# Seven products of quarters for one pair of up-projection columns in four of eight MLP groups, and a planner that writes the order of groups 1 to 6

## The chip, the cores and the metric

The kernel runs on one core of one Trainium2 chip. The metric is the time of one execution in device microseconds (us); shown are the median of three runs and one more run under the hardware profiler.

## The reference, cut to what matters

Two layers work on a residual stream of 512 tokens by 1024 channels in float32. Layer 0 mixes tokens with attention, layer 1 with a short convolution. Each then has the MLP that the change is about, and a gated embedding.

```python
D_MODEL = 1024; SEQ = 512; D_FF = 4 * D_MODEL; DEPTH = 2

def sq_relu_mlp(h, w_up, w_down):
    return jnp.square(jax.nn.relu(h @ w_up)) @ w_down

for i in range(DEPTH):
    ...                                       # mixer, residual
    f = sq_relu_mlp(rmsnorm(x, g[2]), w_mlp_up[i], w_mlp_down[i])
    x = x + rmsnorm(f, g[3])
    ...                                       # gated embedding, residual
```

## The kernel before

**Products.** Each float32 operand is kept as two fp32r halves, a high one (names that end in `h`) and a low one (`l`, the operand minus its high half). `mm3` makes a product from three TensorE matmuls: high by high, low by high, high by low. The normed activations of the MLP stand transposed in SBUF as `hTh` and `hTl`, 8 blocks of 128 channels by 512 tokens.

**Weights.** A weight tile of 128 x 512 comes from HBM into a `raw` buffer (14 of them; SP's queue issues the transfers in the order of one list). ACT casts it to its high half (`wh<-raw`), and DVE or POOL subtracts to get the low half (`wl<-raw,wh`). `prepare` does this for the next 8 entries (`SOON`) of the list `order` ahead of the product that is being written.

**The MLP** of a layer is `mlp`: the 4096 hidden columns go in 8 groups of 512. `up(gr)` makes four blocks `f` of 128 columns, each from 8 x `mm3` over 512 tokens (24 matmuls of 512 columns) into one PSUM bank. ACT then applies relu (`r<-up`) and squares (`q<-r`). `down(gr)` adds the group's share of the down-projection for groups 0 to 6 with Strassen's seven products in Winograd's form. The left operands are quarters of the squared activations and their sums (A11, A12, A22, S1 to S4), of which `quarters` makes the sums on POOL (`s<-q`), and `halves` the high and low halves on ACT and DVE (for blocks 0 and 1, p = 0, and for blocks 2 and 3, p = 1). The right operands are quarters of the weights and their sums (B11, B21, B22, T1 to T4); for groups 1 to 6 DVE makes the sums T in PSUM banks (`dn_T<-...`). Each of the seven products fills two banks (`dn`, 12 matmuls of 512 columns in all), which DVE adds to 14 accumulators in SBUF (`acc<-dn,acc`). `combine` adds these up on POOL after group 6. Group 7 has plain products.

**Seven products elsewhere.** The conv of layer 1 already uses the seven-product form for two of its three projections (`sevens`): there the quarters of the tokens (B11 to B22, T1 to T4) are the moving operand, 256 columns wide, and quarter sums of the weight (S1 to S4, names `c_S`, `b_S`) the stationary one. A pair of 128-column blocks then takes 7 x 4 `mm3`, that is 84 matmuls of 256 columns, where `up` takes 48 of 512.

**Order.** The program writes instructions in the order of its loops, and a scheduler with a timing model of its own then orders each engine's queue, TensorE's (PE's) too. Each engine works its queue in order and waits on semaphores for others.

Of the kernel before, what the change touches and what calls it, by code (L numbers as in the profile page):

```python
# [8 lines left out]
F32 = mybir.dt.float32  # L9
F32R = mybir.dt.float32r  # L10
# [5 lines left out]
P = 128  # L16
# [22 lines left out]
BY_HAND = 8  # L39
LEFT = 10  # L40
LATE = 0
BANKED_FORMS = (
    ("B11", 0), ("T1", 0), ("B11", 1), ("T2", 0), ("B21", 0), ("T4", 0), ("T1", 1), ("T2", 1),
    ("B21", 1), ("T4", 1), ("T3", 0), ("T3", 1), ("B22", 0), ("B22", 1),
)
BANKED = range(1, 7)
DOWN_FORMS = ("B11", "T1", "B21", "T2", "T4", "T3", "B22")
# [16 lines left out]
low_on_pool = lambda key: key[0] == "up"  # L64


class Pair:


    def __init__(self, hi, lo):  # L70
        self.hi, self.lo = hi, lo
# [6 lines left out]
def trunk(ctx: ExitStack, tc, x, xT, pT, g, gT, wv, wqk, bf, wo, wci, wcq, cw, wco, wup, wdn, wpp, wpg, out):  # L78
# [3 lines left out]
    raws = pool("raws", RAWS)  # L82
    normed = pool("normed", 1)
    pages = pool("pages", PAGES)
    small = pool("small", 8)
# [44 lines left out]
    def plan_down(l, gr):  # L130

        plan_sums(
            ("dn", l, gr),
            [
                (PRODUCTS[i][1], p) for i in STEPS for p in range(2)
            ] if gr not in BANKED else BANKED_FORMS,
            [
                ((name, p), wdn[l, c, 4 * gr + 2 * p + r])
                for name, r, c in (("B11", 0, 0), ("B21", 1, 0), ("B12", 0, 1), ("B22", 1, 1))
                for p in range(2)  # L140
            ],
            [
                ((name, p), (a, p), (b, p), ALU.subtract)
                for p in range(2)
                for name, a, b in (("T1", "B12", "B11"), ("T3", "B22", "B12"),
                                   ("T2", "B22", "T1"), ("T4", "B21", "T2"))
            ],
        )

    def plan_sevens(key, srcs):  # L150
        plan_sums(
            key,
            [(f,) for f in QUARTERS],
            [((name,), src) for name, src in zip(("A11", "A12", "A21", "A22"), srcs)],
            [
                ((name,), (a,), (b,), op)
                for name, a, b, op in (
                    ("S1", "A21", "A22", ALU.add), ("S2", "S1", "A11", ALU.subtract),
                    ("S3", "A11", "A21", ALU.subtract), ("S4", "A12", "S2", ALU.subtract),
                )  # L160
            ],
        )
# [80 lines left out]
    for l in range(2):  # L243
        if l == 0:
            for c, (_, width) in enumerate(V_CHUNKS):
                for k in range(KT * width // 512 if width < 272 else KT):
                    plan(("v", c, k), wv[c][k])
            for i in range(KT):
                for j in range(4):
                    plan(("qk", i, j), wqk[i, j])  # L250
            for k in range(KT):
                for n in range(2):
                    plan(("o", n, k), wo[n, k])
        else:
            for s, key in enumerate((("cu", 0), ("b", 0), ("cu", 1))):
                for j in range(4):
                    plan((*key, j), wci[s, j])
            for i in range(2, KT, 2):
                for name in "ucb":
                    s = "cub".index(name)  # L260
                    if name in SEVENS:
                        plan_sevens((name, i), [wcq[i // 2 - 1, s, j] for j in range(4)])
                    else:
                        for j in range(4):
                            plan((name, i, j), wcq[i // 2 - 1, s, j])
            for n in range(2):
                for k in range(KT):
                    plan(("co", n, k), wco[n, k])
        for gr in range(8):
            for i in range(2):  # L270
                for j in range(4):
                    plan(("up", l, 2 * gr + i, j), wup[l, 2 * gr + i, j])
            if gr < 7:
                plan_down(l, gr)
                continue
            for n in range(2):
                for f in range(4):
                    plan(("dn", l, gr, n, f), wdn[l, n, 4 * gr + f])
        for k in range(2):
            plan(("p", l, k), pT[l, :, k, :])  # L280
        for n in range(2):
            for k in range(2):
                plan(("pp", l, n, k), wpp[l, n, k])
        for n in range(2):
            for k in range(KT):
                plan(("pg", l, n, k), wpg[l, n, k])
# [706 lines left out]
    def mlp(l, hT, xs, then, late):  # L993
        acc, lows = {}, {}

        def square(out, r):
            nc.scalar.activation(out, r, AF.Square)  # L997
# [41 lines left out]
        def down(gr, A):  # L1039

            for i in STEPS:
# [9 lines left out]
                for s in range(2):  # L1051
# [3 lines left out]
                    else:  # L1055
                        a = acc[i, s][:, :S]
                        ins = nc.vector.tensor_tensor(out=a, in0=banks[s], in1=a, op=ALU.add)  # L1057
                        if gr == 1:
# [4 lines left out]
                                ),  # L1063
                            )

        def combine():

            for s in range(2):
                for to, i in ((2, 1), (6, 1), (7, 6), (4, 7), (6, 5), (3, 6), (5, 7)):
                    a = acc[to, s][:, :S]  # L1070
                    nc.gpsimd.tensor_tensor(out=a, in0=a, in1=acc[i, s][:, :S], op=ALU.add)  # L1071
            return {
                (2 * half + s, n): acc[i, s]
                for s in range(2) for i, half, n in ((2, 0, 0), (3, 0, 1), (4, 1, 0), (5, 1, 1))
            }

        for gr in range(7):
            A, s, q = {}, {}, {f: page(f"q{l}_{gr}_{f}") for f in range(4)}

            def done(f, lo, hi, r):  # L1080
                square(q[f][:, lo:hi], r[:, : hi - lo])
                if lo == 0 and f % 2 == 0:
                    halves(gr, f, ("A11",), q[f], A)
                if hi == S:
                    quarters(gr, f, q, s, A)

            up(gr, done)
            down(gr, A)

        total, hs, gB = combine(), [], []  # L1090

# [203 lines left out]
def layout(x, p, norm_g, w_attn_in, b_forget, w_attn_out, w_conv_in, conv_w, w_conv_out,  # L1295
           w_mlp_up, w_mlp_down, w_ple_proj, w_ple_gate):

    import numpy as np

    def tiles(w, k, c):  # L1300

        K, C = w.shape
        t = w.reshape(K // (P * k), k, P, C // c, c).transpose(3, 0, 2, 1, 4)
        return t.reshape(C // c, K // (P * k), P, k * c)

    wa = np.asarray(w_attn_in)[0]
# [24 lines left out]
    got["wco"] = tiles(np.asarray(w_conv_out)[0], 1, S)  # L1331
    up, dn = np.asarray(w_mlp_up), np.asarray(w_mlp_down)
    got["wup"] = np.stack([tiles(up[l], 2, 256) for l in range(2)])
# [22 lines left out]
```

## Time and profile before

| | |
|---|---|
| median of 3 runs | 1220.68 us (1220.53 to 1222.57) |
| the profiled execution | 1221.12 us; its span from the first to the last instruction 1219.4 us |
| granted TensorE clock | 0.998 |
| busy: PE, DVE, ACT, POOL | 1206.7, 919.7, 691.0, 512.1 us |
| groups 1 to 6 of the MLP, each | about 40.8 us, in both layers |

Busy time is the time in which an engine has an instruction under way. Matmuls overlap, so their rate is read from the distance of their starts and not from their durations. Consecutive DVE and ACT instructions overlap in the record by about 0.1 us too.

### The profile page before, as it was taken

What the parts mean: (1) busy time and instruction counts of PE and PEld (TensorE: products, weight loads), DVE (VectorE), ACT (ScalarE), POOL (GpSimd) and SP (SyncE); (2) the same over time, 40 slices, a digit from 0 to 9 for tenths busy, and PEclk for the clock granted to TensorE, in tenths of its full rate; (3) what the DMA queues carried; (4) which work ended last, traced back from release to release, by engine and by line L of the source; (5) the groups of instructions that cost most, each with busy time, mean ns of one, the idle gap of its engine ahead of it and who ended that gap; (6) DMA issues with size and microseconds to landing.
All of it is one profiled execution on the core that took longest, in us unless ns stands there. A gap on an engine that the chain in (4) does not pass through costs nothing.

```text
span 1219.4 us, 18413 instructions
## 1 busy us (share of the span) xinstructions
PE 1206.7 (99%) x6175; PEld 1027.7 (84%) x6175; DVE 919.7 (75%) x1570; ACT 691.0 (57%) x1465; POOL 512.1 (42%) x520
## 2 busy tenths in 40 slices
PE   9999999999999999999999999999999999999997
PEld 8888887898888888888889999989888888888886
DVE  7888888584767866799877888866587678669873
ACT  7687778458644554455666533545755445545551
POOL 2035666155534543445213355226554345436210
PEclk9999999999999999999999999999999999999999
DMA  9476554623323423348223123542342234235501
GB/s 324 132 211 170 167 149 126 209 98 88 110 85 112 135 64 105 113 120 286 76 91 111 31 84 105 170 158 70 109 134 72 93 112 138 67 98 175 179 12 58
DMA packets 87310, 150.80 MB, mean 124 GB/s; under 512 B 10352, under 2 KB 18080, under 8 KB 87216
## 3 DMA queue, kind: packets, MB, share of 16 engines
q1 hardware_dynamic: 86640, 149.11, 39.3%
q8 instruction: 48, 0.79, 0.3%
q10 hardware_dynamic: 576, 0.53, 0.1%
q14 instruction: 46, 0.38, 0.1%
HBM read 139.03 MB, written 6.37 MB: 119 GB/s over the span
## 4 chain that ended last, share of the span: by engine, by line
PE 88%; ACT 3%; issue 3%; DVE 2%; POOL 2%; DMA 2%; SPq 0%; POOLq 0%; ACTq 0%; DVEq 0%
PE up L306 9%; PE up L304 9%; PE up L305 9%; PE dn L304 8%; PE dn L306 8%; PE dn L305 8%; PE v L512 3%; PE pg L305 2%; PE pg L304 2%; PE pg L306 2%; PE qk L306 2%; PE qk L305 2%; PE qk L304 2%; PE pT L626 1%; PE co L305 1%
## 5 line engine op out<-in xcount | busy, mean ns | idle before, releaser
L313 DVE TENSOR_TENSOR wl<-raw,wh 128x512 fp32r<-128x512 f32 x250 | 229.5, 949 | 21.3 <-ACT wh L312 20.4
L306 PE MATMUL up<-hTl,wh 128*128 128x512 f32 (+1 forms) x576 | 209.7, 366 | 1.0 <-DVE hTl L313 1.0
L304 PE MATMUL up<-hTh,wh 128*128 128x512 f32 (+1 forms) x576 | 210.3, 366 | 0.0
L305 PE MATMUL up<-hTh,wl 128*128 128x512 f32 (+1 forms) x576 | 210.2, 365 | 0.0
L312 ACT CAST wh<-raw 128x512 fp32r<-128x512 f32 x346 | 193.1, 630 | 4.5 <-DVE xd L409 4.4
L313 POOL TENSOR_TENSOR wl<-raw,wh 128x512 fp32r<-128x512 f32 x96 | 141.0, 1504 | 57.3 <-ACT wh L312 50.0
L306 PEld LDWEIGHTS up<-hTl,wh 128*128 128x128 f32 x576 | 108.3, 189 | 18.7 <-DVE hTl L313 1.2
L305 PEld LDWEIGHTS up<-hTh,wl 128*128 128x128 f32 x576 | 108.6, 189 | 17.6
L304 PEld LDWEIGHTS up<-hTh,wh 128*128 128x128 f32 x576 | 108.6, 189 | 17.5
L312 ACT CAST wh<-dn_T 128x512 fp32r<-128x512 f32 x112 | 61.9, 593 | 100.4 <-DVE dn_T L183 90.0
L1057 DVE TENSOR_TENSOR acc<-dn,acc 128x512 f32<-128x512 f32 x168 | 107.3, 678 | 8.2 <-PE dn L306 8.0
L1011 ACT ACTIVATE r<-up 128x512 f32<-128x512 f32 (+1 forms) x72 | 39.6, 551 | 121.9 <-PE up L306 121.9
L1025 POOL TENSOR_TENSOR s<-q 128x256 f32<-128x256 f32 x28 | 28.2, 1008 | 141.5 <-ACT q L997 139.5
L313 DVE TENSOR_TENSOR wl<-dn_T,wh 128x512 fp32r<-128x512 f32 x112 | 74.6, 692 | 9.4 <-ACT wh L312 9.1
L313 DVE TENSOR_TENSOR A12l<-q,A12h 128x512 fp32r<-128x512 f32 x28 | 19.4, 692 | 73.0 <-ACT A12h L312 73.0
L1071 POOL TENSOR_TENSOR acc<-acc,acc 128x512 f32<-128x512 f32 x28 | 46.5, 1682 | 23.7 <-DVE acc L1057 23.4
L306 PE MATMUL qk<-hTl,wh 128*128 128x512 f32 x128 | 50.6, 396 | 0.0
L305 PE MATMUL pg<-wh,hTl 128*128 128x512 f32 x128 | 50.5, 394 | 0.0
L304 PE MATMUL pg<-wh,hTh 128*128 128x512 f32 x128 | 50.4, 394 | 0.0
L304 PE MATMUL qk<-hTh,wh 128*128 128x512 f32 x128 | 50.3, 393 | 0.0
L305 PE MATMUL qk<-hTh,wl 128*128 128x512 f32 x128 | 50.2, 392 | 0.0
L306 PE MATMUL pg<-wl,hTh 128*128 128x512 f32 x128 | 50.2, 392 | 0.0
(406 smaller groups left out, 3330.6 us busy)
## 6 DMA issues: line engine op xcount, KB each, us to landing
raw<-in_wup SPq DMA_DIRECT2D x128, 256.0 KB, 3.2
raw<-in_wdn SPq DMA_DIRECT2D x128, 256.0 KB, 2.7
raw<-in_wcq SPq DMA_DIRECT2D x36, 256.0 KB, 3.1
raw<-in_wqk SPq DMA_DIRECT2D x32, 256.0 KB, 5.4
raw<-in_wpg SPq DMA_DIRECT2D x32, 256.0 KB, 5.3
g<-in_g SPq DMA_DIRECT2D x22, 256.0 KB, 6.3
prl<-neg_c SPq DMA_DIRECT2D x16, 256.0 KB, 6.3
raw<-in_wo SPq DMA_DIRECT2D x16, 256.0 KB, 4.8
```

The costliest lines, as they stand in the source:

```text
L304: nc.tensor.matmul(ps, a.hi, b.hi, start=start, stop=False)
L305: nc.tensor.matmul(ps, a.lo, b.hi, start=False, stop=False)
L306: nc.tensor.matmul(ps, a.hi, b.lo, start=False, stop=stop)
L312: nc.scalar.copy(hi, src)
L313: return eng.tensor_tensor(out=lo, in0=src, in1=hi.bitcast(F32), op=ALU.subtract)
L512: nc.tensor.matmul(ps[:, : V_CHUNKS[c][1]], getattr(of_x(k, t), p), getattr(ready["v", c, k], of), start=k == 0 and p == of, stop=k == KT ...
L626: nc.tensor.transpose(ps[:, b * P : (b + 1) * P], probs[h][b][:, j * P : (j + 1) * P], ident)
L1011: nc.scalar.activation(r[:, :n], ps[:, :n], AF.Relu)
L1025: sums = lambda out, a, b, op: nc.gpsimd.tensor_tensor(out=out, in0=a, in1=b, op=op)
L1057: ins = nc.vector.tensor_tensor(out=a, in0=banks[s], in1=a, op=ALU.add)
L1071: nc.gpsimd.tensor_tensor(out=a, in0=a, in1=acc[i, s][:, :S], op=ALU.add)
```

## The change

Groups 1 to 6 of each MLP are no longer written by `up` and `down`. A new function, `planned`, enters every step (a product on PE, a cast on ACT, a difference or sum on DVE or POOL, a transfer) into an `Agenda` with a cost, the steps it comes after and, for PE, the clock at which it is due. `Agenda.emit` then lets the engines run against each other by these costs. PE's steps keep their order of entry; on the other engines, of the steps that can start, the one that is due first goes first. The steps are written in that order under `manual_schedule` for PE, DVE, ACT and POOL, so the scheduler no longer orders them. PE's products stand strictly one after the other.

In groups 3 to 6 the first pair of blocks (f = 0 and 1) is made by seven products of quarters (`up_sevens`). Its results come as halves of three banks a, b and c, which DVE adds up (d, v, e, m). The token sums T1 to T4 for it are made once in each layer on POOL from `hT`, and split by ACT and DVE (`tokens_of_sevens`); they are kept in 7 new SBUF pages (`EXTRA`) and 9 of the 70 old ones. The four weight sums for each pair are made on POOL.

For groups 1 to 6 the order in which the down weights come changes too, and T3 is made as T2 minus B11 (one input in PSUM) where it was B22 minus B12 (two inputs in SBUF).

The core of the diff:

```diff
+UP_SEVENS = [(gr, 0) for gr in range(3, 7)]
+UP_PRODUCTS = (
+    ("A11", "B11", "c", 0), ("S2", "T2", "a", 1), ("S1", "T1", "b", 0), ("S3", "T3", "b", 1),
+    ("A12", "B21", "a", 0), ("S4", "B22", "c", 0), ("A22", "T4", "c", 1),
+)
+EXTRA = 7
+LOOK = 14.0
+LOOK_SUMS = 20.0
+SUM_BANKS = 3
+HOP = 0.25
+MARGIN = 2.0
+COSTS = {
+    "PE": (0.0, 0.0), "DVE": (0.07, 1.06e-3), "ACT": (0.17, 0.73e-3), "POOL": (0.15, 2.5e-3),
+    "DMA": (0.0, 1.9e-3),
+}
...
-                for name, a, b in (("T1", "B12", "B11"), ("T3", "B22", "B12"),
+                for name, a, b in (("T1", "B12", "B11"),
+                                   ("T3", "T2", "B11") if gr in BANKED else ("T3", "B22", "B12"),
                                    ("T2", "B22", "T1"), ("T4", "B21", "T2"))
...
+            while any(queues.values()):
...
+                for step in queue[:1] if e in ("PE", "DMA") else queue:
...
+                t = max(free[e], min(r for r, _ in ready))
+                step = min((s for r, s in ready if r <= t + 1e-9), key=lambda s: s.due)
+                wait = max(0.0, port - t) if step.shared else 0.0
...
+            def squared(gr, f, q, name, src, after, uses=()):
...                                       # ACT: relu, then Square
+            def up_sevens(gr, i, A):
...
+                        for k in range(4):
+                            w = ready[(*key, form)].at(lambda u: u[:, k * P : (k + 1) * P])
+                            mm3(ps[s][:, (L, R)[h]], w, second(tokens, k), k == 0, k == 3)
...
+                    at[n] = pe(12 * 0.12, product, [(*key, form)], after, new)
...                                       # after the first product: ACT copies bank c's left half to u
+                d = dve(S, sum_d, (at[4], at["u"]), [rooms["a"]])
+                v = dve(S, sum_v, (d, at[3]))
+                e = dve(256, sum_e, (v,), [rooms["b"]])
+                m = dve(S, sum_m, (v, at[6]), [rooms["c"]])
...
+            def up_plain(gr, i, A):
...
+                        step = pe(6 * 0.227, chunk, [(*key, j)], (), [room] if j == 0 else [])
...
+            def down_planned(gr, A):
+                for i in STEPS:
...
+                        step = pe(6 * 0.227, product, [("dn", l, gr, b_name, p)],
+                                  [low_of[gr, a_name, p]], rooms if p == 0 else [])
...
+            with tc.manual_schedule(engines={
+                mybir.EngineType.PE, mybir.EngineType.DVE, mybir.EngineType.Activation,
+                mybir.EngineType.Pool,
+            }):
+                agenda.emit()
...
-        for gr in range(7):
-            A, s, q = {}, {}, {f: page(f"q{l}_{gr}_{f}") for f in range(4)}
...
+        up(0, done)
+        down(0, A)
+        planned(range(1, 7))
```

**PE, start of the down-projection of group 6, layer 0, before.** In the names, `dn0_6_20` is layer 0, group 6, product 2, bank 0; `A12h0_6_3` is the quarter of blocks 2 and 3 that waits for the last up block (f = 3).

```order
L304 MATMUL dn0_6_50_6670<-wh209_6383,S1h0_6_1_6460 128x512
L305 MATMUL dn0_6_50_6670<-wh209_6383,S1l0_6_1_6461 128x512
L306 MATMUL dn0_6_50_6670<-wl209_6384,S1h0_6_1_6460 128x512
L304 MATMUL dn0_6_50_6670<-wh214_6493,S1h0_6_3_6560 128x512
L305 MATMUL dn0_6_50_6670<-wh214_6493,S1l0_6_3_6561 128x512
L306 MATMUL dn0_6_50_6670<-wl214_6494,S1h0_6_3_6560 128x512
L304 MATMUL dn0_6_20_6600<-wh216_6570,A12h0_6_3_6552 128x512
L305 MATMUL dn0_6_20_6600<-wh216_6570,A12l0_6_3_6553 128x512
```

**The same place now** (the quarter's name is `A12h0_6_2`).

```order
L420 MATMUL dn0_6_20_6960<-wh227_6703,A12h0_6_0_6855 128x512
L421 MATMUL dn0_6_20_6960<-wh227_6703,A12l0_6_0_6856 128x512
L422 MATMUL dn0_6_20_6960<-wl227_6704,A12h0_6_0_6855 128x512
L420 MATMUL dn0_6_21_6961<-wh227_6703,A12h0_6_0_6855 128x512
L421 MATMUL dn0_6_21_6961<-wh227_6703,A12l0_6_0_6856 128x512
L422 MATMUL dn0_6_21_6961<-wl227_6704,A12h0_6_0_6855 128x512
L420 MATMUL dn0_6_20_6960<-wh231_6722,A12h0_6_2_6957 128x512
L421 MATMUL dn0_6_20_6960<-wh231_6722,A12l0_6_2_6958 128x512
```

The second A12 product stood 30 matmuls behind the first down matmul of the group, after half of product 5; now it stands 18 behind.

**ACT, after the last up block of group 6, layer 0, before.** `r` and `q` are relu and square; A12h, S1h, S3h are high halves of left operands, `wh` those of weights.

```order
L1011 ACTIVATE r0_6_3_0_6549<-up0_6_3_0_6524 128x512
L997 ACTIVATE q0_6_3_6353<-r0_6_3_0_6549 128x512
L312 CAST A12h0_6_3_6552<-q0_6_3_6353 128x512
L312 CAST S1h0_6_3_6560<-s120_6_3_6556 128x512
L312 CAST S3h0_6_3_6564<-s340_6_2_6522 128x512
L312 CAST wh216_6570<-raw175_6361 128x512
```

**ACT at the same place now.**

```order
L1315 ACTIVATE rr0_6_3_6940<-up0_6_3_6865 128x512
L1515 CAST wh236_6942<-raw182_6655 128x512
L1319 ACTIVATE qr0_6_3_6951<-rr0_6_3_6940 128x512
L1515 CAST wh237_6954<-raw183_6674 128x512
L1265 CAST A12h0_6_2_6957<-qr0_6_3_6951 128x512
L1515 CAST wh238_6969<-raw184_6684 128x512
L1515 CAST wh239_6975<-raw185_6706 128x512
```

Two weight casts for group 7 now stand between the relu of the last block and the cast of A12 (one in groups 1, 3, 4 and 5, two in groups 2 and 6), and the weights of the group's own products are cast earlier.

**DVE, while group 3 of layer 0 makes its up blocks, before.** `dn_0_3_T2_0` is a weight sum, `wl` a low half of a weight.

```order
L1057 TENSOR_TENSOR acc0_3_1_4308<-dn0_2_31_5099,acc0_3_1_4308 128x512
L313 TENSOR_TENSOR wl145_5182<-dn_0_3_T2_0_5179,wh145_5181 128x512
L183 TENSOR_TENSOR dn_0_3_T4_0_5255<-raw126_5135,dn_0_3_T2_0_5179 128x512
L183 TENSOR_TENSOR dn_0_3_T1_1_5267<-raw129_5141,raw125_5133 128x512
L313 TENSOR_TENSOR A11l0_3_0_5195<-q0_3_0_5126,A11h0_3_0_5194 128x256
```

**DVE at the same place now.** `T3l`, `T4l` are low halves of the token sums, `up_0_6_S4` a weight sum of the seven products; d and v are sums of their results.

```order
L1208 TENSOR_TENSOR acc0_3_1_4311<-dn0_2_31_5206,acc0_3_1_4311 128x512
L1208 TENSOR_TENSOR T3l0_0_4807<-T3f0_0_4804,T3h0_0_4806 128x512
L1208 TENSOR_TENSOR T3l0_1_4823<-T3f0_1_4820,T3h0_1_4822 128x512
L1208 TENSOR_TENSOR wl139_5187<-up_0_6_S4_5153,wh139_5186 128x512
L1208 TENSOR_TENSOR T4l0_0_4882<-T4f0_0_4879,T4h0_0_4881 128x512
L1208 TENSOR_TENSOR T4l0_1_4909<-T4f0_1_4906,T4h0_1_4908 128x512
L1208 TENSOR_TENSOR wl145_5260<-raw124_4970,wh145_5259 128x512
L1208 TENSOR_TENSOR d0_3_0_5333<-up0_3_0a_5243,u0_3_0_5256 128x512
L1208 TENSOR_TENSOR dn_0_3_T1_0_5335<-raw125_5018,raw124_4970 128x512
L1208 TENSOR_TENSOR v0_3_0_5349<-up0_3_0b_5266,d0_3_0_5333 128x512
```

DVE now has eight more instructions in each of groups 3 to 6 (52 where it had 44): four low halves of weight sums and the four sums d, v, e, m. ACT has 43 where it had 38, POOL 19 where it had 16.

More of the change, by code (lines that the diff above doesn't have):

```diff
@@ L84, in trunk @@
     pages = pool("pages", PAGES)
+    extra = pool("extra", EXTRA)
     small = pool("small", 8)
@@ L138, in plan_down @@
                 ((name, p), wdn[l, c, 4 * gr + 2 * p + r])
+                for name, r, c, p in (
+                    ("B11", 0, 0, 0), ("B12", 0, 1, 0), ("B11", 0, 0, 1), ("B22", 1, 1, 0),
+                    ("B21", 1, 0, 0), ("B12", 0, 1, 1), ("B21", 1, 0, 1), ("B22", 1, 1, 1),
+                )
+            ] if gr in BANKED else [
+                ((name, p), wdn[l, c, 4 * gr + 2 * p + r])
                 for name, r, c in (("B11", 0, 0), ("B21", 1, 0), ("B12", 0, 1), ("B22", 1, 1))
@@ L270, in trunk @@
             for i in range(2):
+                tiles = [wup[l, 2 * gr + i, j] for j in range(4)]
+                if (gr, i) in UP_SEVENS:
+                    plan_sevens(("up", l, 2 * gr + i), tiles, UP_FORMS)
+                    continue
                 for j in range(4):
-                    plan(("up", l, 2 * gr + i, j), wup[l, 2 * gr + i, j])
+                    plan(("up", l, 2 * gr + i, j), tiles[j])
             if gr < 7:
@@ L1075, in combine, with done @@
             }
-        for gr in range(7):
-            A, s, q = {}, {}, {f: page(f"q{l}_{gr}_{f}") for f in range(4)}
[L1080 to L1088, printed above, removed]
+        A, s, q = {}, {}, {f: page(f"q{l}_0_{f}") for f in range(4)}
+        def done(f, lo, hi, r):
+            square(q[f][:, lo:hi], r[:, : hi - lo])
+            if lo == 0 and f % 2 == 0:
+                halves(0, f, ("A11",), q[f], A)
+            if hi == S:
+                quarters(0, f, q, s, A)
+        up(0, done)
+        down(0, A)
+        planned(range(1, 7))
         total, hs, gB = combine(), [], []
@@ L1332, in layout @@
     up, dn = np.asarray(w_mlp_up), np.asarray(w_mlp_down)
-    got["wup"] = np.stack([tiles(up[l], 2, 256) for l in range(2)])
+    plain = np.stack([tiles(up[l], 2, 256) for l in range(2)])
+    sevens = up.reshape(2, 2, 4, P, FF // 256, 2, P).transpose(0, 4, 5, 1, 3, 2, 6)
+    is7 = np.array([(i // 2, i % 2) in UP_SEVENS for i in range(FF // 256)])
+    got["wup"] = np.where(is7[:, None, None, None], sevens.reshape(plain.shape), plain)
     got["wdn"] = np.stack([tiles(dn[l], 1, S) for l in range(2)])
```

342 lines of the change are left out of this document (338 added, 4 removed).

## Prediction

> **What bounds the kernel now.** The page comes first: PE is busy for 99% of the span and carries 88% of the chain that ended last.
>
> ```profile
> PE 1206.7 (99%) x6175; PEld 1027.7 (84%) x6175; DVE 919.7 (75%) x1570; ACT 691.0 (57%) x1465; POOL 512.1 (42%) x520
> PE 88%; ACT 3%; issue 3%; DVE 2%; POOL 2%; DMA 2%; SPq 0%; POOLq 0%; ACTq 0%; DVEq 0%
> ```
>
> That is an average, so the second view is busy time by stage. The columns are the stretch, its length, then busy us of PE, PEld, DVE, ACT and POOL. The rows are the end of group 0 with up of group 1, two whole groups, down of group 6 with up of group 7, and group 1's down in layer 1.
>
> ```profile
> 295.00:324.40 29.40, 28.84 (x128) 23.57 (x127) 18.17 (x25) 20.41 (x39) 17.18 (x15) 1.00 0.43 118
> 406.10:446.90 40.80, 40.80 (x182) 33.76 (x181) 29.32 (x46) 20.81 (x39) 19.07 (x16) 1.00 0.33 104
> 487.80:528.60 40.80, 40.80 (x181) 33.75 (x181) 29.32 (x45) 20.82 (x39) 19.07 (x16) 1.00 0.34 104
> 528.60:569.40 40.80, 40.80 (x182) 33.78 (x181) 40.80 (x48) 24.35 (x47) 23.22 (x14) 1.00 0.67 216
> 892.00:933.00 41.00, 40.53 (x179) 33.57 (x180) 29.91 (x44) 20.17 (x38) 19.01 (x16) 1.00 0.34 103
> ```
>
> In a steady group PE never stops and nothing else is full: DVE has 11.5 us idle, ACT 20, POOL 21.7. So new order alone has nothing to win there, and fewer columns on PE shorten the kernel by as much, if the others keep up. The third view, what PE waits for, has in the MLP's groups 1 to 6 only this (us in all, times, longest; one in each layer):
>
> ```profile
> PE dn L304 <- ACT wh L312: 1.1, 2, 0.6
> ```
>
> **Part 1: 48 wide matmuls become 84 narrow ones.** The price is the distance of starts. First and last row of an up pair of 48 wide ones (the last is the first matmul of the next pair), then of a seven-product set in the conv, 84 narrow ones, up to the first of the next set:
>
> ```profile
> 420.06 0.39 PE L304 MATMUL up<-hTh,wh 128*128 128x512 f32 x1
> 430.94 0.39 PE L304 MATMUL up<-hTh,wh 128*128 128x512 f32 x1
> ...
> 693.77 0.28 PE L304 MATMUL c_A<-hTh,wh 128*128 128x256 f32 x1
> 703.84 0.28 PE L304 MATMUL b_A<-hTh,wh 128*128 128x256 f32 x1
> ```
>
> 10.88 us against 10.07 us, so 226.7 and 119.9 ns for each matmul. A pair saves 0.81 us; four groups in two layers make 8 x 0.81 = 6.5 us, all on PE's path. A group of that kind takes 40.8 - 0.8 = 40.0 us. [...]
>
> **Part 2: the wait that goes.** In group 1's down-projection PE stands for a weight cast that ACT has behind the casts of S1 and S3, which wait for POOL:
>
> ```profile
> 322.01 0.62 ACT L312 CAST S1h<-s 128x512 fp32r<-128x512 f32 x1 [1.35 <-POOL s L1025]
> 322.83 0.62 ACT L312 CAST S3h<-s 128x512 fp32r<-128x512 f32 x1 [0.20 <-POOL s L1025]
> 323.36 0.61 ACT L312 CAST wh<-raw 128x512 fp32r<-128x512 f32 x1
> 324.02 0.50 PE L304 MATMUL dn<-wh,A12h 128*128 128x512 f32 x1 [0.56 <-ACT wh L312]
> ```
>
> That weight is now cast while group 1's second up block is made. 2 x 0.56 = 1.1 us go, unless the next late thing takes the place, and that is part 3.
>
> **Part 3: PE can no longer go around a late operand.** The second A12 product stands 18 matmuls behind the first down matmul, 18 x 0.227 = 4.08 us, where it stood 30, 6.8 us. Its chain runs from the last up block over relu, square and cast on ACT to the low half on DVE. The rows of group 3 (first down matmul of PE, then the chain), and five casts in a row as the price of a cast put in between:
>
> ```profile
> 401.00 0.39 PE L304 MATMUL dn<-wh,A11h 128*128 128x512 f32 x1
> 401.20 0.60 ACT L1011 ACTIVATE r<-up 128x512 f32<-128x512 f32 x1 [0.82 <-PE up L306]
> 402.49 0.63 ACT L312 CAST A12h<-q 128x512 fp32r<-128x512 f32 x1
> 403.15 0.69 DVE L313 TENSOR_TENSOR A12l<-q,A12h 128x512 fp32r<-128x512 f32 x1 [0.97 <-ACT A12h L312]
> 402.54 0.74 POOL L1025 TENSOR_TENSOR s<-q,q 128x256 f32<-128x256 f32 x1 [1.25 <-ACT q L997]
> 407.77 2.72 ACT L312 CAST wh<-raw 128x512 fp32r<-128x512 f32 x5
> ```
>
> The low half is done at 403.84, 2.84 us behind 401.00, so 1.24 us are left. A cast costs (2.72 - 0.62) / 4 = 0.53 us. With one in between (groups 1, 3, 4, 5) 0.71 us remain, with two (2 and 6) 0.18. Lower bound of the new wait: 0. Upper bound: the low half and the one ahead of it on DVE are each stretched by 0.5 us (part 4 has the row), so 0.8 us at four places and 0.3 at eight, 5.6 us. I take 0.25 us at the four tight places, 1.0 in all, near the lower end, since the low half above took 0.69 us with POOL at work from 402.54.
>
> Everything else in the down stage has more. S1 of the last pair needs two more POOL sums, and is asked for 42 matmuls, 9.5 us, behind the first.
>
> **Part 4: the eight instructions more on DVE.** Prices in a steady group, and DVE with POOL idle and with POOL full:
>
> ```profile
> L1057 DVE TENSOR_TENSOR acc<-dn,acc 128x512 f32<-128x512 f32 x15 | 9.6, 678 | 1.0 <-PE dn L306 1.0
> L313 DVE TENSOR_TENSOR wl<-raw,wh 128x512 fp32r<-128x512 f32 x6 | 6.2, 1031 | 0.0
> L313 POOL TENSOR_TENSOR wl<-raw,wh 128x512 fp32r<-128x512 f32 x8 | 11.9, 1528 | 4.3 <-ACT wh L312 4.3
> ...
> 538.75 0.68 DVE L313 TENSOR_TENSOR wl<-raw,wh 128x512 fp32r<-128x512 f32 x1
> 542.85 2.38 DVE L313 TENSOR_TENSOR wl<-raw,wh 128x512 fp32r<-128x512 f32 x2
> 411.29 1.87 DVE L1057 TENSOR_TENSOR acc<-dn,acc 128x512 f32<-128x512 f32 x3
> 554.95 3.49 DVE L313 TENSOR_TENSOR wl<-raw,wh 128x512 fp32r<-128x512 f32 x2
> 545.97 17.03 POOL L1071 TENSOR_TENSOR acc<-acc,acc 128x512 f32<-128x512 f32 x10 [1.29 <-DVE acc L1057]
> ```
>
> An instruction with an input in PSUM takes a slot of 0.60 us (three in 1.87 less 0.08 of overlap). One with two inputs in SBUF takes 0.60 alone, and 1.19 to 1.75 while POOL works. Before, 26 of the first kind are 15.6 us; the 18 others share 29.3 - 15.6 = 13.7 us, 0.76 each. Now 31 of the first kind and one of half width make 18.9 us, and there are 20 others. POOL's load rises from 19.1 to 11 x 1.53 + 7.2 = 24.0 us (the four weight sums at the price of its low halves), so I scale the stretch of 0.16 with it to 0.21: 20 x 0.81 = 16.2. DVE: 35.1 of 40.0 us, covered, cost 0. The lower bound is 0 as well. The upper bound is 1.19 us each: 42.7, which is 2.7 us over in each of eight groups.
>
> **Part 5: the rest, each at no cost, with its cover.** ACT gains four casts and a half-width copy, 2.5 us against 20 idle; if it ran out, part 3's chain would be late first. The token sums put 16 POOL instructions of 1.53, 24.5 us, into groups 1 and 2, where POOL has 43 idle, and are first asked for in group 3; without that cover the second product of group 3 waits. Their 8 low halves on DVE are 4.8 to 9.5 us against 23 idle. The low halves of group 7's eight up weights go from DVE to POOL: DVE is full in that stretch (40.80 of 40.80) and is relieved; POOL goes to 23.2 + 12.2 = 35.4 of 40.8. Bytes and transfers stay the same, with the DMA engines a third busy; SP's queue has the down quarters in another order, and all wait for the same 14 buffers. The two adds for a product (1.27 us) stay well inside the 2.72 us in which the next is computed, so banks come free as before. The 9 pages that the token sums hold have no price in the trace: 0 if the other 61 suffice; otherwise it is a wait of ACT or POOL for PE to let go of a weight, which comes in the down stage and shortens the 14 us by which weights are made ahead, so I take 0.
>
> **Sum.** -6.5 - 1.1 + 1.0 = -6.6 us. Against the profiled execution of 1221.12 us (span 1219.4 and 1.7 around it) that is 1214.5; it stands 0.44 above the median of 1220.68, so the forecast is 1214.1 us.
>
> **Rivals.**
>
> *DVE becomes the bound (slower).* The 20 instructions with two SBUF inputs decide it at (40.0 - 18.9) / 20 = 1.06 us each. At 1.19 the time is 1220.7 - 7.6 + 21.6 = 1234.7. For it: 1031 ns for the raw low halves already, and POOL now works 60% of a group, most of it in the down stage. Against: 0.76 as the mean, and DVE full in 528.60:569.40 without a wait of PE. [...] Chance 0.08.
>
> *PE waits at every strict place (slower).* It decides at 7.6 / 12 = 0.63 us for each of 12 groups. At 1.0 us the time is 1225.1; this needs A12 at 5.1 us instead of 2.84 + 0.53. For it: the queues of ACT and DVE are fixed by costs, and one late head holds all behind it. Against: the rows of part 3. Chance 0.07. At 0.4 to 0.8 us the result is 1217.9 to 1222.7, mostly no change: 0.08.
>
> *The narrow matmuls are cheaper here than in the conv.* At the slope alone, (226.7 - 119.9) / 256 = 0.417 ns a column, 84 take 8.97 us, a pair saves 1.91, and the time is 1205.3. Against: 84 in 10.07 us, of the same form. [...] Chance 0.03.
>
> **How the numbers follow.** The forecast's case (1213.1 with no new wait to 1217.9) has 0.74. A measurement of this kernel can tell about 0.2%, 2.4 us, from no change. Faster: 0.74 + 0.03 = 0.77; same: 0.08; slower: 0.08 + 0.07 = 0.15. The range 1212.5 to 1222.0 leaves out the cheap matmuls (0.03), a DVE bound (0.08) and the upper half of the strict waits (0.04).
>
> **What the profile of the changed kernel would show.** Part 1: 84 starts of the new products in 10.07 us, groups 3 to 6 in 40.0 us. Part 2: no wait of PE in group 1's down stage. Part 3: waits of PE for A12's low half in groups 2 and 6 alone, below 0.5 us each. Part 4: DVE busy near 35 of 40 us. PE waiting for accumulator adds or weight low halves in groups 3 to 6 would make the forecast wrong, and so would a busy DVE above 39.

## The result, and the profile after

| | before | changed kernel |
|---|---|---|
| median of 6 runs | 1220.65 us (1220.45 to 1222.57) | 1214.53 us (1213.78 to 1215.43) |
| the profiled execution, its span | 1221.12, 1219.4 us | 1214.68, 1212.9 us |
| ratio of the times | | 0.9947, 95% interval 0.9934 to 0.9960 |

The forecast was 1214.1 us, faster. The page's first part, and the head of its chain:

```profile
PE 1201.4 (99%) x6463; PEld 1035.3 (85%) x6463; DVE 992.4 (82%) x1634; ACT 709.8 (59%) x1513; POOL 625.6 (52%) x592
PE 90%; DVE 3%; issue 2%; ACT 2%; POOL 1%; DMA 1%; SPq 0%; POOLq 0%; DVEq 0%; ACTq 0%
```

PE still bounds the kernel. DVE gained 73 us of busy time and POOL 114. The gain in place comes from the first starts of each stage (PE's timeline of both kernels, layer 0 and layer 1):

| stretch | before | after | difference |
|---|---|---|---|
| start to the MLP of layer 0 | 250.63 | 251.54 | +0.91 |
| group 0 | 46.15, 43.84 | 44.91, 44.28 | -1.24, +0.44 |
| group 1 | 41.66, 41.66 | 41.35, 41.35 | -0.31, -0.31 |
| group 2 | 40.80, 40.82 | 41.00, 41.01 | +0.20, +0.19 |
| groups 3 to 6 | 163.29, 163.27 | 160.08, 160.07 | -3.21, -3.20 |
| group 7 to the MLP of layer 1 | 278.86 | 278.85 | -0.01 |
| group 7 of layer 1 to the end | 108.42 | 108.46 | +0.04 |
| sum | 1219.40 | 1212.90 | -6.50 |

The gain is in groups 1 to 6, 6.64 us in the two layers. Ahead of them the two kernels differ by chance of the start: in the profiles of this study, all with the same instructions there, the MLP of layer 0 begins between 250.57 and 252.64 us. Of the 1.24 us that group 0 of layer 0 gained, 1.02 are a wait of PE for `hTl` that stood in the trace of the kernel before. Group 0 of layer 1 is 0.44 us longer, and that is no chance: it takes 44.22 to 44.30 us in every kernel with the planner (51.01 in pages_66), plain_up included. Late starts at its A12 and S1 make 0.35 of it; why those come late stays open, and the forecast has no term for it.

The same by busy time (stretch, length, busy us of PE, PEld, DVE, ACT and POOL, then clock, DMA share, GB/s), for groups 1 to 6 with group 7's up: before, then after; and one group with seven products, after:

```profile
296.78:564.29 267.51, 266.95 (x1177) 220.69 (x1176) 200.04 (x283) 141.58 (x260) 133.90 (x108) 1.00 0.38 116
```

```profile
296.45:560.64 264.19, 264.14 (x1322) 224.71 (x1320) 240.44 (x321) 150.93 (x284) 189.54 (x144) 1.00 0.41 126
399.78:439.80 40.02, 40.02 (x218) 34.85 (x216) 39.10 (x58) 23.27 (x44) 23.94 (x20) 1.00 0.36 113
```

That group takes 40.02 us as forecast, but DVE is busy for 39.10 of them, not 35.1. The first matmul of its seven products in PE's timeline, and the first of the next pair:

```profile
418.82 0.28 PE L420 MATMUL up_0c<-hTh,wh 128*128 128x256 f32 x1
428.89 0.40 PE L420 MATMUL up<-hTh,wh 128*128 128x512 f32 x1
```

84 starts take 10.07 us, as in the conv. The view of waits names none of PE in the MLP. The distances of starts show what it leaves out, first at group 1's last product (S4 times B22; the tile named S3 holds S3 and S4) with DVE's row for the two low halves of B22, then at group 2's A12 with its low half:

```profile
336.33 0.39 PE L421 MATMUL dn<-wh,S3l 128*128 128x512 f32 x1
336.77 0.50 PE L422 MATMUL dn<-wl,S3h 128*128 128x512 f32 x1
337.11 0.40 PE L420 MATMUL dn<-wh,S3h 128*128 128x512 f32 x1
333.23 3.48 DVE L1208 TENSOR_TENSOR wl<-raw,wh 128x512 fp32r<-128x512 f32 x2
...
363.65 0.39 PE L420 MATMUL dn<-wh,A12h 128*128 128x512 f32 x1
363.94 0.50 PE L421 MATMUL dn<-wh,A12l 128*128 128x512 f32 x1
364.27 0.40 PE L422 MATMUL dn<-wl,A12h 128*128 128x512 f32 x1
362.66 1.22 DVE L1208 TENSOR_TENSOR A12l<-qr,A12h 128x512 fp32r<-128x512 f32 x1
```

A start that should follow after 0.227 us follows after 0.44 and then 0.34: 0.32 us are lost where DVE ends the second low half at 336.71, 1.74 us for each. In group 2, A12's low half takes 1.22 us where it took 0.69 before, and PE loses 0.16 us.

### The profile page after: what moved, and what is told of

The parts are those of the page before. It is cut to its first block, busy times and chain, and to the rows that moved or that the text cites. A ratio compares the mean times of both kernels' runs of the same rounds, so it can differ in the third digit from the quotient of the medians.

```text
span 1212.9 us, 19192 instructions
## 1 busy us (share of the span) xinstructions
PE 1201.4 (99%) x6463; PEld 1035.3 (85%) x6463; DVE 992.4 (82%) x1634; ACT 709.8 (59%) x1513; POOL 625.6 (52%) x592
## 4 chain that ended last, share of the span: by engine, by line
PE 90%; DVE 3%; issue 2%; ACT 2%; POOL 1%; DMA 1%; SPq 0%; POOLq 0%; DVEq 0%; ACTq 0%
PE dn L420 8%; PE dn L422 8%; PE dn L421 8%; PE up L421 6%; PE up L420 6%; PE up L422 6%; PE v L628 3%; PE qk L420 2%; PE qk L422 2%; PE qk L421 2%; PE pg L420 2%; PE pg L421 2%; PE pg L422 2%; PE pT L742 1%; PE co L422 1%
## 5 line engine op out<-in xcount | busy, mean ns | idle before, releaser
L420 PE MATMUL up<-hTh,wh 128*128 128x512 f32 (+1 forms) x448 | 160.7, 359 | 0.0
L421 PE MATMUL up<-hTh,wl 128*128 128x512 f32 (+1 forms) x448 | 160.5, 359 | 0.0
L422 PE MATMUL up<-hTl,wh 128*128 128x512 f32 (+1 forms) x448 | 159.8, 359 | 0.0
L429 DVE TENSOR_TENSOR wl<-raw,wh 128x512 fp32r<-128x512 f32 x162 | 140.5, 908 | 11.2 <-ACT wh L428 10.6
L420 PEld LDWEIGHTS up<-hTh,wh 128*128 128x128 f32 x448 | 84.6, 189 | 12.4
L421 PEld LDWEIGHTS up<-hTh,wl 128*128 128x128 f32 x448 | 84.7, 189 | 12.1
L422 PEld LDWEIGHTS up<-hTl,wh 128*128 128x128 f32 x448 | 84.3, 189 | 12.6
L1208 DVE TENSOR_TENSOR wl<-raw,wh 128x512 fp32r<-128x512 f32 x72 | 71.8, 1009 | 0.0
L1208 DVE TENSOR_TENSOR wl<-dn_T,wh 128x512 fp32r<-128x512 f32 x96 | 63.2, 680 | 1.4 <-ACT wh L1515 1.3
L1208 POOL TENSOR_TENSOR s<-qm,qd 128x256 f32<-128x256 f32 x8 | 6.9, 862 | 90.4 <-ACT qm L1319 71.1
L422 PE MATMUL dn<-wl,S3h 128*128 128x512 f32 x112 | 43.9, 392 | 0.1
```

The source lines that it names most:

```text
L420: nc.tensor.matmul(ps, a.hi, b.hi, start=start, stop=False)
L421: nc.tensor.matmul(ps, a.lo, b.hi, start=False, stop=False)
L422: nc.tensor.matmul(ps, a.hi, b.lo, start=False, stop=stop)
L429: return eng.tensor_tensor(out=lo, in0=src, in1=hi.bitcast(F32), op=ALU.subtract)
L1208: eng.tensor_tensor(out=out, in0=x, in1=y, op=op)
```

## Experiments

The runs ask three things: whether the time is PE's columns and the other engines have room; whether POOL's work lengthens DVE's instructions, and how close DVE is to its end; and whether the written order is what pays. Each expectation has a theory or theories of its own, and a letter in a verdict is that of the run's own expectation. All are measured against the kernel before on the same chip. "Groups" is the length of groups 1 to 6 with group 7's up in layer 0 of the profiled execution, 264.19 us in the changed kernel.

| run | median us | ratio to before (95%) | groups |
|---|---|---|---|
| changed kernel | 1214.53 | 0.9947 (0.9934 to 0.9960) | 264.19 |
| plain_up | 1220.09 | 0.9994 (0.9985 to 1.0002) | 266.56 |
| scheduler_order | 1215.15 | 0.9956 (0.9944 to 0.9969) | 264.49 |
| pool_filled | 1235.03 | 1.0116 (1.0100 to 1.0132) | 270.41 |
| half_filled | 1221.32 | 1.0004 (0.9994 to 1.0014) | 268.09 |
| memset_filled | 1214.93 | 0.9958 (0.9944 to 0.9972) | 264.18 |
| memset_long | 1346.54 | 1.1031 (1.1016 to 1.1046) | 322.90 |
| s_lows_on_pool | 1216.00 | 0.9964 (0.9952 to 0.9976) | 264.97 |
| two_groups_more | 1230.01 | 1.0075 (1.0062 to 1.0088) | 270.78 |
| pages_66 | 1235.02 | 1.0122 (1.0107 to 1.0137) | 264.27 |
| tokens_24 | 1242.48 | 1.0180 (1.0166 to 1.0194) | 277.92 |
| a12_late | 1217.59 | 0.9977 (0.9969 to 0.9986) | 265.71 |
| a12_late_half | 1224.58 | 1.0042 (1.0027 to 1.0057) | 269.13 |

**plain_up: the planner without the seven products.**

```diff
-UP_SEVENS = [(gr, 0) for gr in range(3, 7)]
+UP_SEVENS = []
-            tokens_of_sevens()
+            if UP_SEVENS:
+                tokens_of_sevens()
```

> The planner stays and writes groups 1 to 6 as in the changed kernel, but all up-projection pairs are plain: 48 matmuls of 512 columns, no token sums, nothing of the seven products. Theory A (the time is PE's columns): eight pairs cost 0.81 us more each, 1214.5 + 6.5 = 1221.0 us, less the 0.3 us for each layer that PE stands before its last products in group 1 while POOL makes the token sums, so 1220.4 to 1221.0; groups 3 to 6 take 40.8 us each. Theory B (the order is what pays, the narrow products little): the time stays below 1218. Theory C (eight more DVE instructions and a strict order eat a part of the gain): above 1221.5 would mean that the plain form gives PE more waits than the changed kernel has.

```profile
297.87:564.43 266.56, 266.56 (x1177) 220.79 (x1176) 192.06 (x278) 138.38 (x260) 141.70 (x116) 1.00 0.41 123
```

A, 0.3 us below its range. The planner alone, with the new order of the down weights and the new form of T3, takes 0.95 us off each layer's groups (267.51 to 266.56) and leaves no gap at all, not at the last product of group 1 either; the seven products take off 2.37 more (266.56 to 264.19). Four groups of 40.02 us where plain ones take 40.80 make 3.12, so 0.75 are lost: 0.55 in group 1 and 0.20 in group 2, which take 41.35 and 41.00 us. The median lies only 0.5 below that of the kernel before on this chip; in the profiled execution, the slowest of eleven, the MLP began late (252.64 us).

Group 1 also shows what the token sums do to DVE. Its 15 instructions with two SBUF inputs there take 1.32 us each in the changed kernel, 0.79 in plain_up and 0.80 in tokens_24, and POOL is busy for 37.98 and 25.96 us in the first two. So DVE comes to B22's low halves 36.8 us behind the group's start in the changed kernel, and 25.7 us behind it in plain_up:

```profile
323.59 1.88 DVE L1208 TENSOR_TENSOR wl<-raw,wh 128x512 fp32r<-128x512 f32 x2
```

**scheduler_order: the same steps, the order left to the scheduler.**

```diff
-            with tc.manual_schedule(engines={
-                mybir.EngineType.PE, mybir.EngineType.DVE, mybir.EngineType.Activation,
-                mybir.EngineType.Pool,
-            }):
-                agenda.emit()
+            agenda.emit()
```

> The steps are entered in the planner's order, but without the manual schedule: the scheduler with its own timing model orders the engines' queues again, as it did in the kernel before. The work is the same to the last instruction. Theory A (any order in which nothing is late gives PE's columns): 1213.5 to 1216, with PE's waits below 1 us for each layer. Theory C (the planner's order is needed with DVE at 39 of 40 us): waits of PE for low halves or accumulator adds in several groups, 1217 to 1225.

A. The two ratios' intervals overlap. One wait came back, for a token sum's low half, once in each layer:

```profile
384.15 0.39 PE L422 MATMUL up_0b<-T3l,wh 128*128 128x256 f32 x1 [0.41 <-DVE T3l L1208]
```

**pool_filled and half_filled: more work on POOL, none on DVE.** The first adds this behind each low half that POOL makes for up weights of groups 4 to 7 (29 in each layer), the second has `and key[2] % 2 == 1` besides (16 in each layer):

```diff
+                    if plain_up and key[2] >= 8:
+                        add(idle[:, both], hT.hi[:, 0, :].bitcast(F32), hT.lo[:, 0, :].bitcast(F32),
+                            eng=nc.gpsimd)
```

> The changed kernel with up to 8 POOL additions more in each of the stretches that make the weights of groups 4 to 6 (512 columns, both inputs in SBUF, their result is used by nobody), one behind each low half that POOL makes for these groups' up weights: 8 x 1.53 = 12 us more, POOL at about 36 of 40 us. Nothing is added on DVE. Theory A (DVE's stretched time has room): 1214.5 us within 0.5; DVE's busy time rises to 40 of 40 and PE still does not wait. [...]

> As pool_filled, but only behind the low halves of the plain up pairs' weights, 4 POOL additions more for each of groups 4 to 7 where that kernel had 7 or 8: 6 us more of POOL for each group, 30 of 40. pool_filled took 20.5 us more than the changed kernel, with DVE's two-SBUF instructions at 1.26 us in group 3 where the changed kernel has 0.95. Theory A (DVE has a limit and the stretch is by the share of POOL's time): half the additions bring them to about 1.1 us, 0.15 x 20 = 3 us more DVE in a group, against the 1 to 2 us that DVE has idle: PE begins to wait, 1216 to 1222. Theory B (a threshold that the changed kernel is well below): 1214.5 within 0.5. Theory D (each addition on POOL costs its share, linear): 1214.5 + 10 = 1225.

pool_filled is not A: it takes 20.5 us more than the changed kernel. Its 1235.0 us lie near the 1234.7 of the prediction's rival, but by chance: the groups lose 12.4 of the 20.5 us, 10.5 of them in group 4 alone (groups 3 and 6 lose 0.5 us each, group 5 nothing), where the rival had 2.7 us in each of eight groups. half_filled is A, at the upper end of its range. DVE's groups for the low halves of raw weights in group 3 (count, busy us, mean ns, idle), changed kernel and then pool_filled:

```profile
L1208 DVE TENSOR_TENSOR wl<-raw,wh 128x512 fp32r<-128x512 f32 x7 | 6.7, 954 | 0.0
```

```profile
L1208 DVE TENSOR_TENSOR wl<-raw,wh 128x512 fp32r<-128x512 f32 x6 | 9.0, 1496 | 0.0
440.46:485.71 45.25, 42.19 (x217) 35.90 (x216) 43.37 (x60) 26.08 (x51) 38.16 (x29) 0.96 0.36 106
446.08 0.50 PE L420 MATMUL dn<-wh,A12h 128*128 128x512 f32 x1 [1.38 <-ACT A12h L1265]
448.27 0.50 PE L421 MATMUL dn<-wh,A12l 128*128 128x512 f32 x1 [1.68 <-DVE A12l L1208]
449.52:452.90 3.38, 3.38 (x9) 2.60 (x8) 3.38 (x5) 2.12 (x4) 3.38 (x3) 0.50 0.25 82
```

All of DVE's instructions with two SBUF inputs together have a mean of 0.84 us before (group 3), 0.95, 0.99 and 0.90 in groups 3 to 5 of the changed kernel, 1.12 and 1.06 in groups 3 and 4 of half_filled, 1.26 in group 3 of pool_filled. The prediction's point of decision, a slot of 1.06, is a duration of 1.13 with the 0.07 us that neighbours overlap. half_filled stands there: group 3 still takes 40.02 us with DVE busy for 39.69, and in group 4 PE waits at A12; that group loses 3.8 of the 3.9 us. ACT's fixed order carries the delay on. In the changed kernel the relu of group 4's last block starts 0.20 us behind the group's first down matmul (439.80), in half_filled 2.37 us (440.36), behind weight casts that ran late:

```profile
440.00 0.60 ACT L1315 ACTIVATE rr<-up 128x512 f32<-128x512 f32 x1 [0.31 <-PE up L422]
```

```profile
438.86 0.59 ACT L1516 CAST wh<-dn_T 128x512 fp32r<-128x512 f32 x1 [0.29 <-DVE dn_T L1208]
...
442.73 0.60 ACT L1315 ACTIVATE rr<-up 128x512 f32<-128x512 f32 x1
```

pool_filled loses 6.2 us in each layer's groups; its other 8 us are lost in stages that have none of these additions and that the scheduler orders, the first part of the conv above all (PE waits there for low halves of DVE); why was not separated.

The last row of pool_filled's fence is a second surprise: behind those waits the clock was 0.50 for 3.38 us.

**memset_filled and memset_long: POOL occupied, without reading.**

```diff
+                    if plain_up and key[2] >= 8:
+                        nc.gpsimd.memset(idle[:, both], 0.0)     # memset_long: seven times
```

> As pool_filled, at the same places and in the same number, but POOL writes zeros (512 columns, no input) instead of adding two inputs from SBUF. Theory A (the loss in pool_filled comes from DVE's instructions with two SBUF inputs while POOL reads and writes SBUF): without POOL's reads DVE is stretched less; with a memset shorter than 1 us the time is 1214.5 to 1216. Theory B (the loss comes from POOL's own queue, whose sums and low halves are late behind the additions): the time rises in proportion to the memset's duration, 1225 to 1235 if one takes 1 to 1.5 us.

> As memset_filled, with seven memsets in the place of one: that kernel added 58 of them, 12.9 us of POOL's busy time in all, 0.22 us each, and seven take 1.55 us, as long as one of pool_filled's additions. POOL is as full as in pool_filled and reads nothing for it. [...] Theory B (POOL's queue is late behind whatever is put into it): 1230 to 1236, as pool_filled.

memset_filled is A. The 58 memsets took 0.524 us each (tile view), 30 us of POOL, and cost nothing (264.18); half_filled's 32 additions took 1.74 each, 56 us, and cost 3.9 us in each layer's groups. In proportion the memsets should have cost 2.1, or 1.0 if POOL's busy time is the measure: it rose by 6.6 us in the groups with the memsets, since POOL's own low halves beside them took less (1.32 us, against 1.56 in the changed kernel, from 400 to 480 us), and by 25 with the additions. memset_long's expectation counted 0.22 us a memset, from the rise of POOL's busy time; seven take 3.7, and POOL itself became the bound. Its 1346.5 us are far above its theory's 1230 to 1236, and it doesn't test what it was made for, but its rows tell two things:

```profile
PE up L421 <- POOL wl L1208: 30.5, 10, 9.4
399.19:449.37 50.18, 44.17 (x217) 36.84 (x216) 37.88 (x57) 22.46 (x43) 45.99 (x68) 0.90 0.29 89
L1208 DVE TENSOR_TENSOR wl<-raw,wh 128x512 fp32r<-128x512 f32 x6 | 5.5, 921 | 0.0
```

PE waits for POOL's own results, and with POOL busy for 46 of 50 us DVE's low halves still take 0.92 us, not 1.50. In these runs DVE's stretch went with POOL's reading, not with POOL being busy: the low halves of raw weights in group 3 took 0.95 us in the changed kernel, 1.50 with additions and 0.92 with memset_long's memsets.

**s_lows_on_pool: four low halves in each group from DVE to POOL.**

```diff
-                plain_up = key[0] == "up" and not isinstance(at, tuple)
+                plain_up = key[0] == "up"
```

> The changed kernel with the low halves of the four weight sums of each seven-product pair on POOL instead of DVE: 4 DVE instructions less and 4 POOL instructions more in each of groups 3 to 6. Theory A (DVE's own count is what is scarce): DVE falls from 39 to 36 of 40 us, PE's small waits vanish, 1213.5 to 1214.5. [...]

Not A: 0.8 us more in each layer, though DVE has four instructions less and is busy for 36 of 40 us in group 4. The 16 that are left with two SBUF inputs there take 1.12 us, up from 0.99. The late one, in group 5:

```profile
484.61 0.50 PE L421 MATMUL dn<-wh,A12l 128*128 128x512 f32 x1 [0.46 <-DVE A12l L1208]
```

**two_groups_more: seven products for the second pair too, in groups 5 and 6.**

```diff
-UP_SEVENS = [(gr, 0) for gr in range(3, 7)]
+UP_SEVENS = [(gr, 0) for gr in range(3, 7)] + [(gr, 1) for gr in (5, 6)]
```

> Groups 5 and 6 of each layer make both up pairs by seven products, not the first alone: 4 pairs x 0.81 = 3.2 us less on PE, and in each of the four groups 8 more DVE and 3 more POOL instructions. Theory A (DVE's busy 39 of 40 us in the changed kernel is time stretched by POOL and still has room): 1214.5 - 3.2 = 1211.3 us. Theory B (DVE is at its limit): by the prediction's prices 34.5 DVE instructions with a PSUM input at 0.60 and 24 others at 0.81 make 40.4 us against 39.2 of PE, so 1.2 us more in each of four groups and 1214.5 - 3.2 + 4.8 = 1216.1; with 1.06 us each 46.1 us, and 1214.5 - 3.2 + 27.6 = 1238.9. PE's waits would then be for accumulator adds or low halves made on DVE.

B, between its two numbers. The narrow products keep their price (the stretch from group 4's down to group 5's, now with two such pairs, takes 39.19 us), but in group 6 the operand A11 is late:

```profile
524.34 0.50 PE L420 MATMUL dn<-wh,A11h 128*128 128x512 f32 x1 [3.21 <-ACT A11h L1265]
525.52 0.80 PE L421 MATMUL dn<-wh,A11l 128*128 128x512 f32 x1 [0.68 <-DVE A11l L1208]
```

It isn't DVE's load alone: the sums d, v, e come between the last product and A11, which PE asks for six matmuls after it. Load and chain were not separated.

**pages_66: four SBUF pages fewer.** `PAGES = 66` for 70.

> The changed kernel with 66 SBUF pages instead of 70, nothing else: a measure of what the 9 pages held by the token sums cost, which the prediction put at nothing. Theory A (pages are not scarce in the way that counts): 1214.5 within 0.5. Theory B (a cast that waits for a page holds up ACT's queue, and A12's cast is behind it): four pages fewer shorten the weights' lead and give waits of PE at A12, 1216 or more.

Neither. Groups 1 to 6 don't notice (264.27 against 264.19). The 20 us are lost where the scheduler orders the work, as between group 7's down and the MLP of layer 1, changed kernel and then pages_66:

```profile
560.64:817.73 257.09, 256.81 (x1546) 229.44 (x1545) 200.27 (x304) 131.35 (x287) 78.75 (x78) 1.00 0.34 108
```

```profile
562.35:832.27 269.92, 262.08 (x1545) 232.64 (x1543) 196.20 (x297) 128.84 (x283) 78.19 (x78) 0.98 0.30 98
PE n0b_p L489 <- DVE n0b_h L480: 5.0, 2, 4.0
```

**tokens_24: the token sums 16 us later.** `TOKENS_AT = 24.0` for 8.0.

> The changed kernel, with POOL's token sums begun 24 us into group 1 in the planner's clock and not 8 us. In the changed kernel PE loses 0.3 us in group 1 of each layer before its products with S3, where the low half of a weight takes 1.74 us on DVE while POOL works without a pause. Theory A (the token sums are what stretches it): that loss goes, 1213.9 us; it may come back in group 2, where POOL then has more, so 1213.7 to 1215. Rival (it is the weights' own lateness): the 0.3 us stay, 1214.5.

A for the loss in group 1, and far above all its times for the price. Group 1's down takes 19.04 us, no gap. But the sums come too late for group 3:

```profile
317.95:336.99 19.04, 19.04 (x85) 15.77 (x84) 13.57 (x20) 8.30 (x15) 17.50 (x14) 1.00 0.38 110
378.00:398.00 20.00, 15.85 (x90) 14.16 (x89) 19.61 (x27) 4.88 (x10) 9.40 (x6) 0.74 0.34 106
PE up_0a L422 <- DVE T2l L1208: 1.5, 2, 0.7
```

With the lower clock at such waits (0.74 over 20 us) and the backlog in groups 3 to 5 that makes 13.7 us for each layer.

**a12_late and a12_late_half: more room for A12.** Product 4's first half goes ahead of product 2's second, and DVE takes product 1's banks first; the second run has half_filled's additions too.

```diff
+A12_LATE = ((1, 0), (1, 1), (2, 0), (4, 0), (2, 1), (4, 1)) + tuple(
+    (i, p) for i in (5, 6, 7, 3) for p in range(2))
...
-                for i in STEPS:
+                for i, p in A12_LATE:
...
-                        dve(S, take, (step,), [rooms[s]], due=clock[0] + 3.0)
+                        dve(S, take, (step,), [rooms[s]], due=clock[0] + (0.5 if i == 1 else 3.0))
```

> The changed kernel with the first half of product 4 (A22, T4) ahead of the second half of product 2: A12's second product stands 24 matmuls behind the first down matmul, not 18, so its low half has 1.36 us more. DVE takes product 1's banks first, since six banks would be open and there are five for products. Theory A (the strict place of A12 costs 0.1 to 0.2 us in groups 1 and 2 and nothing elsewhere): 1214.0 to 1214.5. Rival (the banks are the next thing late: product 4 waits for DVE's additions of product 1): up to 1 us in each of twelve groups, 1215 to 1226.

> a12_late with half_filled's 4 POOL additions for each of groups 4 to 7. half_filled lost 2.1 us in group 4 of each layer at A12's second product, and 1.6 us more in the slow matmuls behind that wait. Theory A (DVE's delay is passing, and A12 is only the first to feel it): 1.36 us more room leave 0.7 us of the wait and no slow matmuls, 1216.5 us. Theory B (DVE is short of time for good in that group): whatever room A12 gets is taken by the next operand in the order, and the time stays at 1220 to 1222.

a12_late has the time of its rival, but not the rival's wait: it is slower by 1.5 us in each layer, and PE waits for low halves, not for banks. The gaps in groups 1 and 2 are gone, and others have come in groups 3 and 5. Group 3, PE and DVE:

```profile
405.36 0.50 PE L423 MATMUL dn<-wh,A12l 128*128 128x512 f32 x1 [0.55 <-DVE A12l L1210]
409.96 0.50 PE L423 MATMUL dn<-wh,S1l 128*128 128x512 f32 x1 [0.19 <-DVE S1l L1210]
402.61 1.27 DVE L1210 TENSOR_TENSOR acc<-dn,acc 128x512 f32<-128x512 f32 x2
403.81 1.50 DVE L1210 TENSOR_TENSOR A12l<-qr,A12h 128x512 fp32r<-128x512 f32 x1
```

The two additions that free the banks now stand ahead of A12's low half on DVE and use up the room. With POOL's additions the loss is the same as without the new order (1224.58 - 1217.59 = 7.0, against 1221.32 - 1214.53 = 6.8), and most of it has moved to S1's low half (2.4 of 3.4 us of waits in layer 0): B, though 1224.58 us lie above its range, as a12_late does above the changed kernel. None of the variants beats the changed kernel.

## Why the prediction was right, and where its steps were off

**Part 1, right.** 10.07 us for 84 narrow matmuls, 40.02 us for a group, 6.41 us in eight groups where 6.5 were forecast (6.24 against plain_up).

**Part 2, right and too small.** The wait is gone. It cost more than the 0.56 us in its row: from 323.07 to 324.36 PE made two starts in 1.29 us where it needs 0.45, so 0.84 us. plain_up shows 0.95 for all that the order gains in a layer's groups. The term was 1.1 and should have been 1.7 to 1.9.

**Part 3, right in mechanism, off in place and size.** A12's low half, stretched by POOL, is late in group 2 (0.16 us) and hardly in group 1 (0.1); in group 6, with its two casts in between, not at all. The forecast had 1.0 us at four places; A12 costs about 0.5 in all.

**Part 5, the step that failed.** The token sums stood at no cost, with 43 us of POOL's idle time as cover. Idle time of POOL was no cover for DVE: in group 1 its instructions with two SBUF inputs go from 0.79 to 1.32 us, about 8 us in all, and B22's second low half comes 0.3 us late. Beside those two low halves POOL makes low halves of its own, not token sums; the sums' part is that DVE gets to them so late. plain_up and tokens_24 show that gap gone when the sums are not there. With A12's part the seven products lose 0.75 us in groups 1 and 2 of each layer, 1.5 in all against the forecast's 1.0. Nor is the cover wide: 16 us later in the plan is too late. The pages, put at nothing as well, cost nothing within the groups (pages_66).

**Part 4, the cost right, its size not.** DVE was to be busy for 35.1 of 40.0 us and is for 37.7 to 39.1. The step that failed is the scaling of the stretch with POOL's load: 0.84 us for an instruction with two SBUF inputs became 0.90 to 0.99, not 0.88 (0.81 with the overlap taken off). The count is the other part: 53 to 57 instructions start in these groups, not 52. It cost nothing only because it stayed below 1.13. The sign that the prediction named, DVE busy above 39, came in group 3 without any wait of PE: there a stretched DVE was busy for 39.10 of 40.02 us and still in time.

**The sum.** With plain_up in between, the groups give -1.9 for the order, -6.2 for the pairs and +1.5 for the late operands, -6.6 in all, and the rest of the span +0.1. The forecast was -6.5 - 1.1 + 1.0. That it came so near is in part luck: two terms were too small with opposite signs, and the 0.44 us of layer 1's group 0 went unseen beside 1.02 us of a wait that was gone. The rival "DVE becomes the bound" did not occur, but 0.08 was a low chance for it: about 7 us more of reading work on POOL in a group make PE wait in one group of a layer, nearly twice as much in three.

## What to carry to other kernels

When work is moved to an engine with idle time, price it by what it does to the instructions of the other engines (POOL's token sums went with 1.32 us for DVE's with two SBUF inputs in group 1, 0.79 without them), and by the margin of those engines' next deadlines; the share of idle time told neither here. Take the cost of a wait from the distance of starts around it: the row of the wait in the kernel before left out a third of it (0.56 of 0.84 us), and behind two waits of 2.1 us together half_filled's clock was 0.50 for 3.40 us. A kernel that runs without waits can stand a few us from a cliff (7 us of additions on POOL in a group cost half_filled 6.8 us in all), and adding idle work at one engine shows how far.

## What was not expected of the hardware

Behind waits that add up to 2.1 us the granted TensorE clock was 0.50 for 3.40 us. In half_filled PE's starts at A12 were 0.59 and 1.49 us late within 2.5 us, and then came:

```profile
445.04 0.49 PE L420 MATMUL dn<-wh,A12h 128*128 128x512 f32 x1 [0.43 <-ACT A12h L1265]
446.76 0.54 PE L421 MATMUL dn<-wh,A12l 128*128 128x512 f32 x1 [1.23 <-DVE A12l L1208]
447.10:450.50 3.40, 3.40 (x9) 2.65 (x8) 3.40 (x6) 1.92 (x4) 3.40 (x5) 0.50 0.13 45
```

From 447.10 to 450.50 eight starts stood 0.425 us apart, and 0.227 in a steady group, which is 1.6 us lost on top of 2.1 waited. Waits of the same sum came without it too. In group 5 of two_groups_more PE is late for A12 in both layers. Over the two rows of layer 0 it is idle for 1.18 and 0.42 us, over the two of layer 1 for 1.60 and 0, and only in layer 1 is the second row at half clock (two rows of layer 0, two of layer 1):

```profile
477.38:480.79 3.41, 2.23 (x14) 1.63 (x12) 3.41 (x5) 2.65 (x6) 3.13 (x3) 1.00 0.22 77
480.79:484.20 3.41, 2.99 (x12) 2.25 (x13) 3.36 (x6) 3.41 (x9) 2.71 (x4) 1.00 0.00 0
1050.82:1054.23 3.41, 1.81 (x7) 0.94 (x7) 3.41 (x5) 3.38 (x7) 2.44 (x3) 1.00 0.04 13
1054.23:1057.64 3.41, 3.41 (x10) 2.65 (x9) 3.37 (x6) 3.12 (x7) 3.41 (x4) 0.50 0.00 0
```

So 1.60 us of idle PE within 6.8 us came with the half clock for 3.41 us and without it, and no run shows what decides. Executions of one kernel differ as well: of half_filled's ten, the two of 1218.5 and 1218.7 us had a mean granted clock of 0.999, the five of 1221.8 to 1223.1 us one of 0.996.
